# Spreading gamma's load over sixteen partitions in an RMSNorm and swish kernel

## The chip, the cores and the metric

The kernel runs on one core of a Trainium2 chip. The metric is the time of one execution on the device in microseconds (us), as a median of several runs. The profile's span is about 1.8 us shorter than the time.

## The reference

```python
batch, seq, dim = 16, 1024, 512            # x ~ N(0,1), gamma = ones(512), eps = 1e-5
def reference(x, gamma, eps):
    rms = np.sqrt(np.mean(x ** 2, axis=-1, keepdims=True) + eps)
    x_norm = x / rms * gamma
    return (x_norm * (1.0 / (1.0 + np.exp(-x_norm)))).astype(np.float32)
```

That is 33.5 MB read and 33.5 MB written, with little arithmetic. Gamma is one row of 2 KB. It is all ones here.

## The kernel before

Sixteen rows per partition fill a 4 MB load, after three smaller loads. SyncE issues the loads of x, ScalarE issues gamma's load and the stores. VectorE multiplies by gamma, for which every partition needs a copy of it. Gamma is loaded into four partitions, the first of each group of 32, and a shuffle on VectorE copies each group's first partition to the other 31.

```python
    sizes = [4, 4, 8] + [16] * 6 + [8, 8]          # rows per partition of each load
    ...
    def load(t):                                                             # line 70
        nc.sync.dma_start(out=buf(t), in_=dram(xf, t))
    def store(t):                                                            # line 73
        nc.scalar.dma_start(out=dram(of, t), in_=buf(t))
    ...  # sums(k): squares on ScalarE (line 80, 3 rows of 4) and VectorE (line 86)
    ...  # root(k): VectorE (line 93), then pow on GpSimd (line 97)
    ...  # norm(k): x * rstd * gamma_sb on VectorE (line 104)
    ...  # swish(k): Silu of 4 rows on ScalarE (line 111)
    with tc.manual_schedule():
        nc.gpsimd.memset(gamma4[:], 0.0)                                     # line 114
        nc.gpsimd.memset(neg_half[:], -0.5)
        nc.scalar.dma_start(out=gamma4[0:P:32, :], in_=gamma.partition_broadcast(4))   # 116
        nc.scalar.preload_act_table_set("silu_and_others")                   # line 117
        ...  # loads of the first 32 rows are issued
        for k in range(K + 3):
            if k < K:
                sums(k); root(k)
            ...  # stores that are due
            if k == 0:
                nc.vector.stream_shuffle(gamma_sb[:], gamma4[:], [0] * 32)   # line 140
            if 1 <= k <= K:
                norm(k - 1)
            ...  # swish(k - 2), and the next loads
```

## Time and profile before

| | before |
|---|---|
| time, median | 163.06 us (162.83 to 163.09, 3 runs) |
| span of the profiled run | 161.1 us |
| moved by DMA, both ways | 67.15 MB, 417 GB/s over the span |
| VectorE / ScalarE busy | 69% / 74% |
| ScalarE's last instruction (a store's issue) | starts at 146.8 us |

These lines of the page of the kernel before show the load on the DMA engines. The row of digits is the busy share of the DMA engines in tenths in 40 slices of the span; the lines of q1 (loads of x) and q10 (stores and gamma) give packets (the pieces that the trace records of a transfer), MB and the share of the 16 engines' span.

```profile
span 161.1 us, 612 instructions
...
DMA  5999989999899999999999999999999999999993
...
DMA packets 3180, 67.15 MB, mean 417 GB/s; under 512 B 356, under 2 KB 356, under 8 KB 360
...
q1 hardware_dynamic: 1584, 33.56, 49.1%
q10 hardware_dynamic: 1592, 33.56, 48.4%
```

The two queues together fill 97.5% of the 16 engines' time, and only the ends of the span and two slices at 8 fall short. The kernel is bound by DMA; compute fits beneath it. The packets count too: q10 has eight more than q1, gamma's four pieces of data and four semaphore updates, which report that data has landed.

The first 13 us of the kernel before, in order of time (start, duration, both in us, then the instruction; in brackets, idle time of its engine before it and what ended it):

```profile
1.29 1.08 ACTq L116 DMA_DIRECT2D gamma<-in_gamma_dram  x1
2.40 1.28 ACT L117 ACT_TABLE_LOAD   x1 [2.40 <-issue]
5.54 0.63 ACT L80 ACTIVATE junk_a<-xb 128x512 bf16<-128x512 f32 x1 [1.85 <-DMA xb<-in_x_dram]
...
7.63 0.72 DVE L140 STREAM_SHUFFLE gamma_sb<-gamma 128x512 f32<-128x512 f32 x1
...
8.09 0.63 ACT L80 ACTIVATE junk_a<-xb 128x512 bf16<-128x512 f32 x1 [0.60 <-DMA xb<-in_x_dram]
...
12.98 0.63 ACT L80 ACTIVATE junk_a<-xb 128x512 bf16<-128x512 f32 x1 [2.94 <-DMA xb<-in_x_dram]
```

Gamma's issue takes 1.08 us of ScalarE's sequencer. The shuffle, which needs gamma, starts at 7.63 us. The three lines of junk_a, which waited, are the first pieces of the first three loads: the first load of x is seen at 5.54 us, the second at 8.09, the third at 12.98. (In a line, "junk_a<-xb" names the tile written and the tile read.) So the gap between the first and the second load is 2.55 us; gamma's packets run among those of the second load.

The chain that ended last, in shares of the span:

```profile
## 4 chain that ended last, share of the span: by engine, by line
DMA 59%; ACT 20%; another core or an unknown queue 4%; issue 4%; DVE 3%; SPq 1%; DVEq 0%; ACTq 0%
```

### The profile page before, as it was taken

The page shows a single profiled execution, that of the slowest core. Times are in us where ns is not written, and L with a number is a line of the kernel's source. Part 1 is how long each engine was busy: PE and PEld are TensorE (multiplying, and loading weights), DVE is VectorE, ACT ScalarE, POOL GpSimd, SP SyncE. Part 2 cuts the span into 40 slices and gives each one's busy share as a digit, 9 for nine tenths or more (in the row PEclk, how much of TensorE's full clock was granted, in tenths as well). Part 3 has the DMA queues.
Part 4 walks back from the last instruction along what each step waited for, and adds up shares of the span by engine and source line. Part 5 has one row for each costly group of instructions (what it writes and reads, how often), then busy time and mean ns, then how long its engine had stood idle before and what let it go on. Part 6 is the DMA issues. An engine that isn't in the chain of part 4 may idle for free.

```text
span 161.1 us, 612 instructions
## 1 busy us (share of the span) xinstructions
DVE 110.7 (69%) x226; ACT 118.7 (74%) x225; POOL 46.4 (29%) x38
## 2 busy tenths in 40 slices
DVE  0376946998999999999966998069999604990000
ACT  3447919999999999999939996099999408954000
POOL 1052403333444433333333333033333302400000
DMA  5999989999899999999999999999999999999993
GB/s 171 437 435 521 390 352 488 413 403 480 366 407 431 484 411 447 399 456 447 399 447 456 399 439 464 417 415 421 431 435 464 419 403 472 415 415 423 439 415 146
DMA packets 3180, 67.15 MB, mean 417 GB/s; under 512 B 356, under 2 KB 356, under 8 KB 360
## 3 DMA queue, kind: packets, MB, share of 16 engines
q1 hardware_dynamic: 1584, 33.56, 49.1%
q10 hardware_dynamic: 1592, 33.56, 48.4%
q14 instruction: 4, 0.03, 0.0%
HBM read 33.56 MB, written 33.55 MB: 417 GB/s over the span
## 4 chain that ended last, share of the span: by engine, by line
DMA 59%; ACT 20%; another core or an unknown queue 4%; issue 4%; DVE 3%; SPq 1%; DVEq 0%; ACTq 0%
DMA xb<-in_x_dram 41%; DMA out_dram<-xb 19%; ACT junk_a L80 12%; ACT xb L111 8%; DVE xb L104 3%; SPq L70 1%; DVEq L178 0%; DVE aeps L93 0%; ACTq L80 0%
## 5 line engine op out<-in xcount | busy, mean ns | idle before, releaser
L104 DVE SCALAR_TENSOR_TENSOR xb<-xb,rstd,gamma_sb 128x512 f32<-128x512 f32 x128 | 87.4, 745 | 0.0
L80 ACT ACTIVATE junk_a<-xb 128x512 bf16<-128x512 f32 x96 | 59.0, 615 | 23.9 <-DMA xb<-in_x_dram 23.9
L97 POOL TENSOR_TENSOR rstd<-aeps,neg_half 128x4 f32<-128x4 f32 x32 | 45.6, 1426 | 94.1 <-DVE aeps L93 94.1
L111 ACT ACTIVATE xb<-xb 128x2048 f32<-128x2048 f32 x32 | 60.7, 1896 | 1.8 <-DVE xb L104 1.8
L86 DVE CUSTOM_DVE_ANT_0 junk_v<-xb 128x512 bf16<-128x512 f32 x32 | 21.9, 685 | 19.6 <-DMA xb<-in_x_dram 19.6
L80 ACT ACTIVATION_READ_ACCUMULATOR junk_a<-xb 128x1 f32 x96 | 18.0, 187 | 0.0
L93 DVE TENSOR_SCALAR aeps<-ms 128x4 f32<-128x4 f32 x32 | 5.4, 170 | 14.5 <-ACT junk_a L80 14.5
L117 ACT ACT_TABLE_LOAD x1 | 1.3, 1283 | 2.4 <-issue 2.4
L86 DVE DVE_READ_ACCUMULATOR2_ANT ms<- 128x1 f32 x32 | 2.6, 82 | 0.0
L140 DVE STREAM_SHUFFLE gamma_sb<-gamma 128x512 f32<-128x512 f32 x1 | 0.7, 725 | 0.0
L114 POOL MEMSET gamma<- 128x512 f32 x1 | 0.5, 524 | 0.3 <-POOLq L164 0.3
L164 POOL MEMSET const-float32-0.0<- 128x1 f32 x1 | 0.1, 98 | 0.2 <-issue 0.2
L164 POOL MEMSET const-bfloat16-1.0<- 128x1 bf16 x1 | 0.1, 101 | 0.0
L164 POOL MEMSET const-uint8-127<- 128x1 uint8 x1 | 0.1, 101 | 0.0
L115 POOL MEMSET neg_half<- 128x4 f32 x1 | 0.1, 101 | 0.0
L164 POOL MEMSET const-float32-1.0<- 128x1 f32 x1 | 0.1, 98 | 0.0
L140 DVE LOAD_MASK_SELECT gamma_sb<-gamma x1 | 0.0, 14 | 0.0
## 6 DMA issues: line engine op xcount, KB each, us to landing
xb<-in_x_dram SPq DMA_DIRECT2D x6, 4096.0 KB, 43.8
out_dram<-xb ACTq DMA_DIRECT2D x6, 4096.0 KB, 34.6
xb<-in_x_dram SPq DMA_DIRECT2D x3, 2048.0 KB, 38.8
out_dram<-xb ACTq DMA_DIRECT2D x3, 2048.0 KB, 13.9
xb<-in_x_dram SPq DMA_DIRECT2D x2, 1024.0 KB, 5.8
out_dram<-xb ACTq DMA_DIRECT2D x2, 1024.0 KB, 19.7
gamma<-in_gamma_dram ACTq DMA_DIRECT2D x1, 8.0 KB
```

The lines of the kernel that those rows point to most:

```text
L70: nc.sync.dma_start(out=buf(t), in_=dram(xf, t))
L80: nc.scalar.activation(out=junk[:], in_=row, func=AF.Square, accum_out=ms[:, k, j : j + 1],)
L86: nc.vector.tensor_tensor_reduce(out=junk[:], in0=row, in1=row, scale=1.0, scalar=0.0, op0=ALU.mult, op1=ALU.add, accum_out=ms[:, k, j : j ...
L93: nc.vector.tensor_scalar(out=aeps[:, k, :], in0=ms[:, k, :], scalar1=inv_d, scalar2=eps_f, op0=ALU.mult, op1=ALU.add,)
L97: nc.gpsimd.tensor_tensor(out=rstd[:, k, :], in0=aeps[:, k, :], in1=neg_half[:], op=ALU.pow)
L104: nc.vector.scalar_tensor_tensor(out=row, in0=row, scalar=rstd[:, k, j : j + 1], in1=gamma_sb[:], op0=ALU.mult, op1=ALU.mult,)
L111: nc.scalar.activation(out=rows, in_=rows, func=AF.Silu)
L114: nc.gpsimd.memset(gamma4[:], 0.0)
L115: nc.gpsimd.memset(neg_half[:], -0.5)
L117: nc.scalar.preload_act_table_set("silu_and_others")
L140: nc.vector.stream_shuffle(gamma_sb[:], gamma4[:], [0] * 32)
L164: nc = _bacc.Bacc("TRN2", target_bir_lowering=False, num_devices=1)
```

## The change

Gamma goes to every eighth partition, sixteen in all. The shuffle still takes the first partition of each group of 32, so twelve of the sixteen rows are never read. Why one would try it: with sixteen rows the transfer can use all sixteen DMA engines. The Trainium skill ("DMA: Bandwidth & Descriptors", Rules for kernel authors, "Use all 16 engines") warns that a leading broadcast of fewer than 16 copies confines a DMA to that many engines; the trace agrees, with four semaphore packets for four copies. (The tile's name changes with it.)

```diff
-        nc.gpsimd.memset(gamma4[:], 0.0)
+        nc.gpsimd.memset(gamma16[:], 0.0)
         nc.gpsimd.memset(neg_half[:], -0.5)
-        nc.scalar.dma_start(out=gamma4[0:P:32, :], in_=gamma.partition_broadcast(4))
+        nc.scalar.dma_start(out=gamma16[0:P:8, :], in_=gamma.partition_broadcast(16))
...
-                nc.vector.stream_shuffle(gamma_sb[:], gamma4[:], [0] * 32)
+                nc.vector.stream_shuffle(gamma_sb[:], gamma16[:], [0] * 32)
```

More of the change, by code (lines that the diff above doesn't have):

```diff
@@ L50 @@
     xb = pool.tile([P, ring, D], fp32, name="xb")
-    gamma4 = pool.tile([P, D], fp32, name="gamma4")
+    gamma16 = pool.tile([P, D], fp32, name="gamma16")
     gamma_sb = pool.tile([P, D], fp32, name="gamma_sb")
```

## The prediction

> **What bounds the kernel now.** The DMA engines. The page gives a span of 161.1 us with 67.15 MB moved at a mean of 417 GB/s; in the row of busy tenths the DMA has 9 in 36 of 40 slices. The loads' queue took 49.1% and the stores' queue 48.4% of the 16 engines' span. VectorE is busy 69%, ScalarE 74%. The chain that ended last is 59% DMA. After ScalarE's last instruction (a store issued at 146.8 us) only stores drain, at about 430 GB/s, to the end.
>
> **What the change does.** One DMA, issued by ScalarE at 1.3 us, writes 16 rows of 2 KB and not 4. Every other instruction stays, in the same order on each engine. The shuffle takes row 0 of each 32, so 12 of the 16 rows are never used: the result is right, and nothing is saved downstream.
>
> **What it adds.** The stores' queue had 1592 packets and the loads' 1584: the 8 extra are gamma's four data and four semaphore packets. The Trainium skill ("DMA: Bandwidth & Descriptors", Why a DMA increments its semaphore by 16 and not by 1) says that a DMA from ScalarE runs on the largest number of engines up to 16 that divides the outer dimension, here 4; the trace agrees with its four and four packets. So the new one runs on all 16: 1616 packets in that queue.
> In the trace's DMA records each 2 KB packet took 84 ns and each semaphore packet 9 ns (an 8 KB packet of x 309 ns). So 12 x 93 ns = 1.1 us of engine time is added, 0.07 us when shared by 16, or 0.093 us on each engine that had none. If the slowest engine of a load was one of the four, nothing is added; otherwise up to 0.09 us. My estimate: +0.05 us.
>
> **Critical path.** The shuffle is not held up by gamma: gamma's packets ran about 5.8 to 6.0 us from the span's start and their semaphores landed by 6.3 us, while the shuffle started at 7.63 us, behind the first scaling of the sums, which waited for ScalarE's squares. Slack 1.3 us. The issue on ScalarE took 1.085 us, the table load ran 2.40 to 3.68 us, and ScalarE then idled 1.85 us for x; an issue some tenths longer would be hidden. What is on the critical path is the 0.09 us by which the second load of x (seen at 8.09 us), among whose packets gamma's sit, may come later; the engines are full from there to the end, so that is not won back.
>
> **Prediction.** 163.06 + 0.05 = 163.1 us; range 162.7 to 163.6, mostly the spread of runs (162.83 to 163.09) and small shifts of when loads and stores meet. Chances: faster by over 2% 0.01, within 2% 0.98, slower by over 2% 0.01.
>
> **What would show each step.** Stores' queue 1616 packets, packets under 2 KB 368 (356 + 12). Gamma's issue 1.0 to 1.4 us. Shuffle at about 7.6 us, not waiting for gamma. Second load seen by ScalarE at 8.1 to 8.25 us. Gamma's packets 84 ns. DMA share and GB/s unchanged, and the drain after about 147 us as long as before.
>
> **What would make it wrong.** Sixteen reads of the same 2 KB at once could each take far longer than 84 ns and hold up x's packets on all engines. The issue could grow with the rows and delay gamma past 7.6 us; but loads for 32 rows have already been issued, so only a delay of several us would reach the end. Or a small shift of one store changes how loads and stores interleave, worth perhaps 0.5 us either way.

## The result, and the profile after

| | before | after |
|---|---|---|
| time, median of 4 runs | 163.07 us (162.83 to 163.09) | 163.25 us (163.19 to 163.55) |
| ratio | | 1.0018, 95% interval 1.0001 to 1.0035 |
| packets of the stores' queue | 1592 | 1616 |
| gamma's issue on ScalarE | 1.08 us | 0.62 us |
| first / second load of x seen by ScalarE | 5.54 / 8.09 us | 5.66 / 8.33 us |
| shuffle starts | 7.63 us | 7.75 us |

"Within 2%" was right, and the time lies in the range.

The same lines of the page after:

```profile
span 161.4 us, 612 instructions
...
DMA  5999989999999999999999999999999999999992
...
DMA packets 3204, 67.18 MB, mean 416 GB/s; under 512 B 368, under 2 KB 368, under 8 KB 384
...
q1 hardware_dynamic: 1584, 33.56, 49.1%
q10 hardware_dynamic: 1616, 33.59, 48.4%
```

The 24 more packets are there, with gamma's 0.03 MB more, and nothing else in the totals moves beyond the spread of runs. Now the first 13 us after the change:

```profile
1.29 0.62 ACTq L116 DMA_DIRECT2D gamma<-in_gamma_dram  x1
1.93 1.28 ACT L117 ACT_TABLE_LOAD   x1 [1.93 <-POOL neg_half L115]
...
5.66 0.63 ACT L80 ACTIVATE junk_a<-xb 128x512 bf16<-128x512 f32 x1 [2.44 <-DMA xb<-in_x_dram]
...
7.75 0.72 DVE L140 STREAM_SHUFFLE gamma_sb<-gamma 128x512 f32<-128x512 f32 x1
...
8.33 0.63 ACT L80 ACTIVATE junk_a<-xb 128x512 bf16<-128x512 f32 x1 [0.73 <-DMA xb<-in_x_dram]
...
13.21 0.63 ACT L80 ACTIVATE junk_a<-xb 128x512 bf16<-128x512 f32 x1 [2.93 <-DMA xb<-in_x_dram]
```

Three things are to be seen. The issue became shorter, not longer. The shuffle moved by 0.12 us, with the first load, on whose squares it follows; gamma did not hold it. And the second load came 2.67 us after the first, not 2.55.

The chain that ended last, after the change:

```profile
## 4 chain that ended last, share of the span: by engine, by line
DMA 40%; ACT 38%; another core or an unknown queue 4%; issue 4%; DVE 3%; SPq 1%; DVEq 0%; ACTq 0%
```

This line looks as if 19% of the span had gone from DMA to ScalarE. It had not. Near 61 us the issue of a load waits both for a store and for ScalarE, which come almost together, and the chain follows the later one (in the changed kernel's view of waits, ScalarE ended that wait, of 0.3 us). The changed kernel run again (e9_after below) has the old shares:

```profile
## 4 chain that ended last, share of the span: by engine, by line
DMA 59%; ACT 21%; another core or an unknown queue 4%; DVE 3%; issue 2%; SPq 1%; DVEq 0%; ACTq 0%
```

And e12_next4, which loads four rows as the kernel before does, has 40% and 38%. A kernel's chain can take either branch at a tie; it says nothing of the change.

### The profile page after: what moved, and what is told of

Read it like the earlier page. It is cut to its first block, busy times and chain, and to the rows that moved or that the text cites. A ratio compares the mean times of both kernels' runs of the same rounds, so it can differ in the third digit from the quotient of the medians.

```text
span 161.4 us, 612 instructions
## 1 busy us (share of the span) xinstructions
DVE 110.7 (69%) x226; ACT 118.7 (74%) x225; POOL 46.4 (29%) x38
## 3 DMA queue, kind: packets, MB, share of 16 engines
q10 hardware_dynamic: 1616, 33.59, 48.4%
## 4 chain that ended last, share of the span: by engine, by line
DMA 40%; ACT 38%; another core or an unknown queue 4%; issue 4%; DVE 3%; SPq 1%; DVEq 0%; ACTq 0%
DMA xb<-in_x_dram 40%; ACT junk_a L80 21%; ACT xb L111 17%; DVE xb L104 3%; SPq L70 1%; DVEq L178 0%; DVE aeps L93 0%; ACTq L80 0%
```

## The experiments

Five theories were to be told apart, and they go by letters.

- W (work): a load ends with its slowest engine, and the change puts 93 ns of packets on twelve engines that had none.
- S (same row): sixteen engines that read one and the same row of 2 KB also slow x's own packets.
- Q (queue): a packet of another queue on each engine does that, whatever it reads. D (destination): where the rows land decides.
- N (noise): none of it shows.

As the time moves by a tenth of a per cent, three marks from the trace were used beside it. All come from one profile of each run:

- *gap*: when ScalarE sees the second load of x, less when it sees the first; the start's own jitter (5.54 to 5.67 us over all runs) drops out.
- *moved*: KB of x and of the output (not of gamma) moved between 6 and 10 us from the span's start, worked out from the DMA records, a packet's bytes spread evenly over its duration. The full rate is 433 KB a us (in this mark a KB is 1000 bytes).
- *stretched*: how many of the 8 KB packets of x that start after 5.5 us took over 340 ns; they take 309 undisturbed.

The last two marks, and the times of gamma's packets in the prediction, count from a point 0.24 us before the origin of the timelines shown here: 6 to 10 us is 5.76 to 9.76 there, and 5.5 is 5.26. On the timelines' own axis, from 6 to 10 us, the changed kernel's three profiles move 28 to 48 KB less than before, sixteen different rows 3 KB less and gamma in 128 rows 666 and 679 KB less, and the stretched packets are 8, 9 and 13, none and one, and 65 and 69. The sizes depend on the window; the order doesn't.

The twelve runs and the first two profiles (the time is that of the run's own comparison):

| run | gamma's rows | issue us | gap us | moved KB | stretched | ratio to before (95%) |
|---|---|---|---|---|---|---|
| before | 4, every 32nd | 1.08 | 2.55 | 1718 | 0 | 1 |
| e1_same | the same | 1.08 | 2.54 | 1708 | 1 | 1.0000 (0.9984 to 1.0015) |
| e8_nogamma | none | none | 2.54 | 1717 | 0 | 0.9988 (0.9973 to 1.0003) |
| e12_next4 | 4 adjacent | 0.56 | 2.53 | 1717 | 0 | 0.9991 (0.9971 to 1.0011) |
| e3_rows8 | 8, every 16th | 1.16 | 2.68 | 1712 | 0 | 0.9999 (0.9985 to 1.0013) |
| after | 16, every 8th | 0.62 | 2.67 | 1639 | 9 | 1.0018 (1.0001 to 1.0035) |
| e2_after | the same | 0.61 | 2.92 | 1669 | 9 | 1.0007 (0.9992 to 1.0022) |
| e9_after | the same | 0.61 | 2.87 | 1647 | 15 | 0.9998 (0.9979 to 1.0016) |
| e7_next16 | 16 adjacent | 0.39 | 2.79 | 1668 | 16 | 1.0023 (0.9995 to 1.0052) |
| e5_other16 | 16 rows of x | 0.61 | 2.66 | 1707 | 0 | 0.9991 (0.9977 to 1.0005) |
| e10_other16 | the same | 0.62 | 2.75 | 1705 | 2 | 1.0005 (0.9988 to 1.0022) |
| e4_rows128 | 128 | 0.38 | 4.25 | 1026 | 66 | 1.0061 (1.0047 to 1.0074) |
| e11_rows128 | the same | 0.39 | 4.32 | 1005 | 75 | 1.0065 (1.0050 to 1.0080) |
| e6_other128 | 128 rows of x | 0.38 | 3.21 | 1459 | 1 | 1.0026 (1.0013 to 1.0040) |

### e1_same: the kernel before against itself

No edit.

> The kernel before, unchanged, timed against itself: the noise of the comparison. All theories: ratio 1.000, within 0.1% (0.16 us). In the profile, the issue of gamma 1.0 to 1.2 us again; ScalarE sees the first load of x at 5.54 us and the second at 8.09 us, both within 0.05 us, if those two places repeat from run to run. If they move by 0.1 us or more between two profiles of one kernel, the 0.12 us and 0.24 us by which they came later after the change prove nothing.

Measured: ratio 1.0000, with a half width of 0.15% from five runs (162.80 to 163.71 us). The issue was 1.08 us, the loads were seen at 5.62 and 8.16 us. Each place moved by 0.07 to 0.08 us, more than the 0.05 expected, but both together: the gap stayed at 2.54. So the first load's 0.12 us after the change is not to be read, and the gap is.

### e2_after and e9_after: the changed kernel again

No edit.

> The changed kernel again. Theory W (a load ends with its slowest engine, and the change puts 93 ns of packets on 12 engines that had none): +0.05 to +0.09 us, ratio 1.0003 to 1.0006. Theory S (sixteen engines that read the same 2 KB, or sixteen gamma streams in flight, also slow x's own packets at the start): +0.15 to +0.3 us, ratio 1.001 to 1.002, as the first comparison gave (1.0018). Theory N (noise): as e1_same. All: issue of gamma about 0.62 us, not 1.085.

> The changed kernel a third time, on the chip of the next two, for a direct comparison. Bytes of x moved from 6 to 10 us from the span's start have so far fallen behind the kernel before by 0.18 and 0.11 us in its two profiles (in us at 430 GB/s), and by 0.00 to 0.02 us with no gamma, with 8 rows, with 16 different rows and in the kernel before run again. Theory S: 0.1 to 0.2 us again, some of x's packets between 6 and 8 us over 340 ns, second load seen at 8.25 to 8.55 us; time 0.1 to 0.3 us above before. If those two profiles were chance: 0.00 to 0.05 us. Issue 0.62 us.

Measured: ratios 1.0007 and 0.9998. With the first comparison that is +0.29, +0.11 and -0.03 us (ratio less 1, times 163), a mean of +0.13 us; the interval of the first comparison alone left out 1, those of the others include it. The marks in the trace repeat better than the time: the second load was seen at 8.54 and 8.51 us, the gap was 2.92 and 2.87 us, and from 6 to 10 us 49 and 71 KB fewer were moved than before (79 in the first profile); at 430 KB a us that is 0.11 to 0.18 us for the three. Nine, nine and fifteen packets of x were stretched. So a small cost does arise at this place each time. In the time it is at the edge of what can be seen, and what S expected there (+0.15 to +0.3 us, then +0.1 to +0.3) did not come in either repeat.

### e3_rows8: eight rows

```diff
-        nc.scalar.dma_start(out=gamma4[0:P:32, :], in_=gamma.partition_broadcast(4))
+        nc.scalar.dma_start(out=gamma4[0:P:16, :], in_=gamma.partition_broadcast(8))
```

> Gamma to 8 partitions. Packets: stores' queue 1584 + 8 + 8 = 1600. W: between 0 and +0.09 us. S: about half of what 16 rows cost, +0.07 to +0.15 us. Issue time of gamma: if it shrinks with the number of engines left over (16 - k[...]), 1.085 us at 12 left over and 0.62 us at none give 39 ns each, so 0.93 us here with 8 left over; if it only depends on whether k is 16, 1.085 us.

Measured: ratio 0.9999, 1600 packets, no stretched packet, 6 KB fewer moved. The cost does not begin in proportion to the rows, as S had it: eight readers show none. The gap of 2.68 us is 0.13 more than before, near the 0.093 us of a gamma packet and its semaphore on an engine without slack. The issue took 1.16 us, not 0.93: the idea that the issuing engine pays 39 ns for each engine left out is wrong.

### e4_rows128 and e11_rows128: gamma to all partitions

```diff
-        nc.scalar.dma_start(out=gamma4[0:P:32, :], in_=gamma.partition_broadcast(4))
+        nc.scalar.dma_start(out=gamma4[0:P:1, :], in_=gamma.partition_broadcast(128))
```

> Gamma to all 128 partitions (the shuffle stays): 8 data packets of 84 ns and one semaphore packet on each engine, 0.68 us where four engines had 0.093. W: +0.59 to +0.68 us, ratio about 1.004. S: well over that, +1 us or more, with packets of gamma or of x longer than 84 and 309 ns among them. N, or if the engines had slack: within 0.1%. Stores' queue 1584 + 128 + 16 = 1728 packets, unless several rows are put in one packet. Issue about 0.6 us if it depends on engines left over, longer if it grows with rows.

> 128 rows of gamma again. With one row read by all it fell behind by 1.61 us from 6 to 10 us, with 128 different rows by 0.61. Theory S: 1.5 to 1.7 us behind again; then, as the first time, some of that comes back by 25 us, where the kernel before has its own slump (333 to 416 KB a us at 19 to 22 us, where the full rate is 433), and the time ends 0.9 to 1.1 us over before. If nothing could be won back: 1.6 us over before.

Measured: ratios 1.0061 and 1.0065, about +1.0 us (164.03 and 164.20 us), where packets alone give 0.59 to 0.68 us. W alone is too small. The issue took 0.38 us, not the 0.6 expected. In this fence of e4_rows128's timeline the second load comes at 9.84 us, 4.25 us after the first:

```profile
5.59 0.63 ACT L80 ACTIVATE junk_a<-xb 128x512 bf16<-128x512 f32 x1 [2.60 <-DMA xb<-in_x_dram]
...
9.84 0.63 ACT L80 ACTIVATE junk_a<-xb 128x512 bf16<-128x512 f32 x1 [2.31 <-DMA xb<-in_x_dram]
...
10.11 0.72 DVE L140 STREAM_SHUFFLE gamma_sb<-gamma 128x512 f32<-128x512 f32 x1
```

The shuffle waited for gamma here, until 10.11 us. That seems to have done no harm of its own: at 158 us the bytes moved lagged behind the kernel before by 0.96 us, which is the whole of the time lost. From 6 to 10 us 692 and 713 KB fewer were moved, 1.6 us at 430 KB a us, which is more than the time lost at the end. The rest was won back. These are stretches of the span, first of the kernel before, then of e4_rows128; the columns are us, busy time of VectorE, ScalarE and GpSimd with their instructions, clock, DMA share and GB/s. (This view books a packet's bytes where it starts, so it is rougher than the table.)

```profile
core 0: us, DVE busy (x) ACT busy (x) POOL busy (x), PEclk, DMA share, GB/s
...
6.00:10.00 4.00, 1.65 (x7) 3.40 (x12) 1.01 (x1) 1.00 1.08 463
...
19.00:23.00 4.00, 2.41 (x4) 1.36 (x1) 1.28 (x1) 1.00 0.88 328
```

```profile
core 0: us, DVE busy (x) ACT busy (x) POOL busy (x), PEclk, DMA share, GB/s
...
6.00:10.00 4.00, 0.46 (x3) 1.70 (x7) 1.01 (x1) 1.00 0.98 341
...
19.00:23.00 4.00, 3.79 (x8) 3.15 (x7) 1.44 (x1) 1.00 1.06 459
```

The kernel before has a slump of its own from 19 to 23 us, 328 GB/s, just when loads of x go on alone and the first stores begin; in e4_rows128 that stretch ran at 459. By the finer count the kernel before moved 1524 KB there and both runs of 128 rows 1734, which is 0.49 us won back. A second place is 45 to 49 us: 1632 KB before, 1729 in both, 0.23 us. Together: 1.6 less 0.49 less 0.23 is 0.9 us, which with 0.1 us of a later start is the 1.0 us found. Only the first place is clearly due to the delay: from 19 to 23 us all other profiles moved 1498 to 1558 KB, that of e6_other128, with over a third of the delay, among them. From 45 to 49 us they ranged from 1603 to 1725 KB, so the 0.23 us may be chance. Why the slumps come and why a later stream misses them was not tested.

### e5_other16, e10_other16: sixteen different rows

Wrong result on purpose, from the changed kernel:

```diff
-        nc.scalar.dma_start(out=gamma16[0:P:8, :], in_=gamma.partition_broadcast(16))
+        nc.scalar.dma_start(out=gamma16[0:P:8, :], in_=xf[R - 16 : R, :])
```

> Wrong result on purpose: the sixteen rows of 2 KB come from sixteen different rows of x (its last ones), not all from the one row gamma; all else as the changed kernel. In the two profiles of the changed kernel, after 16 rows of gamma some of x's packets took 340 to 520 ns and not 309, and the second load of x was seen at 8.33 and 8.54 us (before: 8.09 and 8.16). If reading one row sixteen times at once is what stretches them (theory S): here no stretched packets behind the sixteen, second load seen at 8.1 to 8.25 us (each engine's own 93 ns at most). If it is having a packet of another queue on each engine, whatever it reads (theory Q): 8.3 to 8.5 us again. Time: S ratio 1.000 to 1.0006, Q 1.0007 to 1.0018. Issue about 0.6 us if the engines or the destination's step decide it.

> Sixteen different rows of x again (wrong on purpose), on the same chip as the changed kernel. Theory S: falls behind by 0.00 to 0.07 us from 6 to 10 us, no x packet stretched behind the sixteen, second load at 8.1 to 8.3 us; time within 0.1% of before and 0.1 to 0.2 us under the changed kernel. Rival (chance): no order between this and the changed kernel.

Measured: none and two packets of x stretched, 11 and 13 KB fewer moved (0.03 us), against 9 to 16 stretched and 49 to 79 KB fewer in the four profiles where sixteen read gamma's one row. Issue, packets and destination are the same; only the source differs. That speaks for S and against Q. One rival stays open: no run read one row of x sixteen times, so that it is the sharing of a row, and not something about gamma's own place in memory, is not shown; eight reads at that place (e3_rows8) stretched nothing. The gap tells less: 2.66 and 2.75 us here, 2.67 to 2.92 with one row, so they overlap, and 0.11 to 0.20 us over before is somewhat more than the packets' 0.093. The second run saw the second load at 8.42 us, past its expected 8.1 to 8.3, having started at 5.67. In time the two kinds are not told apart: 0.9991 and 1.0005, and on the same chip e10_other16 (163.17 us) came out above e9_after (163.01), against the order expected. The difference of about 0.1 us lies below what five rounds show.

### e6_other128: 128 different rows

Wrong result on purpose, from the changed kernel:

```diff
-        nc.scalar.dma_start(out=gamma16[0:P:8, :], in_=gamma.partition_broadcast(16))
+        nc.scalar.dma_start(out=gamma16[:], in_=xf[R - 128 : R, :])
```

> Wrong result on purpose: 128 different rows of x to 128 partitions, against 128 times gamma, which cost 1.0 us (ratio 1.0061) and had its second load seen at 9.84 us, with x's packets of 400 to 540 ns and gamma's up to 225 ns. Theory S (one row read by all): packets 84 and 309 ns again, second load seen at 8.7 to 8.9 us (8 x 84 + 9 = 0.68 us later), time +0.6 us or less (the bytes alone: 256 KB more than 8), ratio up to 1.004. Theory Q: ratio 1.006, second load at 9.8 us, packets stretched as before.

Measured: ratio 1.0026, +0.43 us (1.0061 and 1.0065 with one row read 128 times, and the intervals don't meet). All 128 packets took 84 ns; one packet of x was stretched, not 66 or 75; the second load was seen at 8.88 us:

```profile
5.67 0.63 ACT L80 ACTIVATE junk_a<-xb 128x512 bf16<-128x512 f32 x1 [2.69 <-DMA xb<-in_x_dram]
...
8.88 0.63 ACT L80 ACTIVATE junk_a<-xb 128x512 bf16<-128x512 f32 x1 [1.26 <-DMA xb<-in_x_dram]
...
9.38 0.72 DVE L140 STREAM_SHUFFLE gamma_sb<-gamma 128x512 f32<-128x512 f32 x1
```

The gap of 3.21 us is 0.66 over before, as eight packets and a semaphore (0.68 us) on each engine give. At this size what S forecast is clear of noise: as many bytes from gamma's one row cost about 0.6 us more than from different rows of x.

### e7_next16: sixteen adjacent partitions

From the changed kernel:

```diff
-        nc.gpsimd.memset(gamma16[:], 0.0)
+        nc.gpsimd.memset(gamma16[:], 1.0)
-        nc.scalar.dma_start(out=gamma16[0:P:8, :], in_=gamma.partition_broadcast(16))
+        nc.scalar.dma_start(out=gamma16[0:16, :], in_=gamma.partition_broadcast(16))
```

> Sixteen rows of gamma to the adjacent partitions 0 to 15 and not to every eighth one (the tile is preset to 1.0, so the result is right only because this gamma is all ones). Issue of gamma: 0.38 us, as with 128 adjacent partitions, if the step of the partitions makes it long; 0.62 us if the number of rows per engine does. Theory S: second load as late as in the changed kernel, 8.3 to 8.55 us, time within 0.1% of the changed kernel's, since the source is the same; if where the rows land mattered (theory D, destination), it would differ by more than 0.15 us from that.

Measured: sixteen stretched packets, 50 KB fewer moved, gap 2.79 us, within what the changed kernel shows. The destination does not matter to it (against D). The ratio of 1.0023 has an interval of 0.9995 to 1.0052, as two of its six runs were high (163.75 and 164.58 us); its median is 163.26. The issue took 0.39 us, so the step between partitions, not the number of rows per engine, makes it 0.62 in the changed kernel.

### e8_nogamma: no transfer at all

```diff
-        nc.gpsimd.memset(gamma4[:], 0.0)
+        nc.gpsimd.memset(gamma4[:], 1.0)
-        nc.scalar.dma_start(out=gamma4[0:P:32, :], in_=gamma.partition_broadcast(4))
```

> No transfer of gamma (its tile preset to 1.0; right only because this gamma is all ones): what the transfer costs in all, and the most that any other way of sending gamma could win. Four rows cost nothing that shows, if their four engines had slack: time within 0.1% of before (W, S), second load seen at 8.05 to 8.2 us. If gamma's transfer cost what the sum of its packets says on the slowest engine: 0.09 us less, not separable from noise either.

Measured: ratio 0.9988, interval 0.9973 to 1.0003; gap 2.54 us, 1717 KB moved, as with four rows. The time is 0.2 us lower, just past the 0.1% expected, but within noise. So the four rows of before cost nothing that shows. That their four engines had slack in the second load fits this, but is argued: the records do not name the engine. The sixteen semaphore packets of that load came over 0.23 us in the kernel before and over 0.51 us in e1_same, so some engines were done that much earlier than others. The run also bounds what sending gamma in another way can save: no more than the whole transfer costs, by the interval at most 0.27% (0.44 us).

### e12_next4: four adjacent partitions

```diff
-        nc.gpsimd.memset(gamma4[:], 0.0)
+        nc.gpsimd.memset(gamma4[:], 1.0)
-        nc.scalar.dma_start(out=gamma4[0:P:32, :], in_=gamma.partition_broadcast(4))
+        nc.scalar.dma_start(out=gamma4[0:4, :], in_=gamma.partition_broadcast(4))
```

> What made gamma's issue 1.085 us with 4 rows, 1.16 with 8, 0.62 with 16, 0.39 with 16 adjacent. Four rows to the adjacent partitions 0 to 3 (preset to 1.0; right only because gamma is all ones). If a step between partitions costs about 0.23 us and using under 16 engines about 0.5 us, each on its own: 0.85 us. If the step alone decides: 0.39 us. If the number of engines alone: 1.08 us. Time as before within 0.1%, whichever: ScalarE waits for x after it anyway.

Measured: issue 0.56 us, which none of the three rules gave. Adjacent rows issue in 0.56 us with four and 0.39 with sixteen; stepped ones in 1.08 with four, 1.16 with eight and 0.62 with sixteen. Both the step and having fewer than sixteen rows lengthen it, and together they add more than each alone. What the sequencer does in that time stays open. The time, 0.9991 of before, is the same.

## Why the prediction was right

- **What bounds the kernel: right.** DMA fills the span in all profiles, and the time followed the data stream alone. In e4_rows128 the shuffle waited until 10.11 us, and the time lost was no more than the stream's lag.
- **The drain: right.** From ScalarE's last instruction to the end it is 14.3 us before (146.8 to 161.1) and after (147.1 to 161.4).
- **What is added: the count was right.** 1616 packets in the stores' queue and 368 under 2 KB, gamma's packets at 84 ns (in e2_after one at 98 and in e9_after one at 107).
- **The shuffle does not wait for gamma: right.** 7.63 to 7.76 us with four, eight or sixteen rows, following the first load. The slack was 1.6 us rather than 1.3: the prediction set the packets' times 0.24 us too late beside the shuffle's.
- **Gamma's issue "1.0 to 1.4 us": wrong.** It fell to 0.62 us. The prediction took it to stay or to grow with the rows. It cost nothing, since ScalarE idles until x comes, as was said.
- **The cost on the second load: the mechanism was right, the term too small.** It was put at up to 0.09 us, with the load seen at 8.1 to 8.25 us; it was seen at 8.33, 8.54 and 8.51. Part of that is the later first load; the gap, which leaves this out, grew by 0.12, 0.37 and 0.32 us. The prediction counted the new packets' own time and took x's packets to stay at 309 ns. Some took up to 521 when sixteen engines read gamma's one row, and with sixteen different rows at most two were stretched. That danger was named among what would make the prediction wrong, and it occurred, but at a small size: 0.11 to 0.18 us by the bytes moved, where packets from sixteen different rows lost 0.03.
- **"The engines are full from there to the end, so that is not won back": wrong as a rule.** With 128 rows, of 1.6 us lost at the start 0.7 us came back by the end, 0.5 of it in the slump from 19 to 23 us. With sixteen rows, the lag behind the kernel before's profile at 158 us was 0.20, 0.21 and 0.09 us, and the kernel before run again lagged by 0.12 itself. What is left of so small a delay at the end was not to be told from chance.
- **The total: +0.05 us predicted.** Measured: +0.29 us by the first ratio, 0.18 by its medians, +0.13 as the mean of three comparisons. The forecast of no visible change holds. The range, 0.4 us down and 0.5 us up, is wide beside all of these, so that the time fell into it does not test the +0.05; the exact size is not settled by these runs, as a comparison of five rounds is good to about 0.25 us.

Settled is that reading gamma's one row by all engines slows other traffic more than reading as many different rows (e4_rows128 and e11_rows128 against e6_other128); that it does so with sixteen readers is shown by the stretched packets and the bytes moved, not by the time. By what mechanism was not tested.

## What to carry to other kernels

In a kernel bound by DMA, cost a small extra transfer as engine time, and look whether its engines have slack in the load it runs among: the four of this kernel cost nothing that showed. Spreading a broadcast over all engines is no gain by itself when its landing gates nothing, and a broadcast load in which all engines read the same row can slow the other traffic; load few copies and spread them on chip. When an effect is near the noise, measure the place where it arises (a gap, bytes moved, packet durations) and enlarge it (128 rows) before believing a ratio.

## What the Trainium skill lacked or had wrong

- "DMA: Bandwidth & Descriptors", Rules for kernel authors, "Use all 16 engines", tells that a broadcast of c copies is confined to c engines, and nothing of what many engines reading one row cost. Here 128 copies of one 2 KB row cost 1.0 us and 128 different rows 0.43 us; x's 8 KB packets beside the former took up to 572 ns where 309 is usual. With 8 copies nothing of it shows.
- The same page has no trn2 figure for the issue time of a small DMA from ScalarE by shape. Here: 1.08 us (4 rows, every 32nd partition), 1.16 (8, every 16th), 0.62 (16, every 8th), 0.56 (4 adjacent), 0.39 (16 adjacent), 0.38 (128).
- The same page, Where 436 GB/s comes from, says that between HBM and SBUF the HBM side (about 358 GB/s) binds. As a rule for every case that is too strong: this core, with 417 GB/s over its span and 433 KB a us in its full stretches, ran near the 435 GB/s that the section gives for the fabric, and the section itself calls a measured 425 GB/s near that rate. What the core beside it did is not on record here.
- No page tells of slumps of the stream such as that from 19 to 23 us (1524 KB where the full rate gives 1732); their cause is open.
